# RWKV-7 key norms as a two-part float32r product, with the norm's scale put into B

## The chip, the cores and the metric

The kernel runs on one core of a Trainium2 chip. The metric is the device time of one execution in microseconds. The kernel before took 2318.72 us, the median of 3 runs (2318.38 to 2319.49). PE is the matrix engine, DVE the vector engine, ACT the scalar engine, POOL and SP the other two; PEld stands for PE's weight loads. Products that the code makes in float32r carry the label f32 in the profile; the kernel splits such an operand into two float32r parts, "hi" (a cast) and "lo" (what the cast left over).

## The reference, cut to what matters

A layer of 1024 tokens by 2048 features: an RMS norm, one input projection, two groups of heads (RWKV-7 and HGRN2), one output projection, a residual and a last RMS norm. The change lies in the RWKV-7 group, 16 heads of 64 channels:

```python
kk = (k * k_k).reshape(B, T, H, N)
kk = kk / jnp.maximum(jnp.linalg.norm(kk, axis=-1, keepdims=True), 1e-12)
k = k * (1.0 + (a - 1.0) * k_a)
...
avec = -kk
bvec = kk * a4

def step(S, inp):
    rt, wt, kt, vt, at, bt = inp
    Sa = jnp.einsum('bhvk,bhk->bhv', S, at)
    S = S * wt[:, :, None, :] + Sa[..., None] * bt[:, :, None, :] + vt[..., None] * kt[:, :, None, :]
    y = jnp.einsum('bhvk,bhk->bhv', S, rt)
    return S, y
```

In the product of avec and bvec the norm of kk appears squared: 1/max(|kk|², 1e-24) per token and head, times -1. The kernel keeps kk without its norm and applies that one factor somewhere, with another factor 0.5 because sigmoid is made from tanh: a = (1 + tanh)/2.

## The kernel before, in words

**Tiling.** Activations lie with features on the 128 partitions and tokens along the free dimension, 512 tokens ("half" 0 and 1) at a time. A tile of 128 partitions holds two RWKV heads, so the 16 heads are 8 pairs `i`, and each part below runs 16 times (8 pairs, 2 halves). 512 tokens are 8 chunks of 64.

**The product that everything else rides on.** `gemm` makes one block of 128 output columns of the input projection: 16 slices of the contraction, three matmuls each (lines 780, 781, 782: hi by hi, hi by lo, lo by hi). Weights come by DMA (`raw`), ACT casts them (`whi`, line 743) and DVE subtracts (`wlo`, line 753), three parts of four slices ahead of use. After each slice, that is after every three matmuls, `gemm` calls `step()`, which lets every waiting lane run up to its next `yield`. So the order of the instructions on each engine is written out by the counts of yields (the constants F00 to F06 and R00 to R20): a "step" is three matmuls of the projection plus what the lanes put behind them. Each pair takes 8 blocks, K, R, V, four for HGRN2 and the RWKV gate, which is 128 steps. Pair 0 of each half has two blocks more, for the low-rank inputs.

**The lane `front`** (`rwkv_front`) is queued when block K is taken out of PSUM, and starts three steps later (six steps after the second low-rank block for pair 0). I count its steps as f0, f1 and so on:

- f0: ACT makes `kk` (line 427) and its square `ksq` (429).
- f1: PE makes the decay product `pz` with `product` (line 188, three matmuls), ACT its tanh (435); then PE makes the squared norms `pn` with four plain float32 matmuls (439) in which the weights are slices of `ksq` and the moving operand is two columns of the block matrix, so that the tokens come out on partitions.
- f2: DVE adds 1 (444) and makes the cumulative sum `G` over each chunk (449).
- f4: PE makes the rate product (188, three matmuls), ACT its tanh `tha` (454); DVE makes `D2`, -2/max(norm², 1e-24), 128 partitions by 8 columns (458 four times, 459).
- f5: ACT makes `Em` (462) and `km` (464). f7: DVE line 466. f9: DVE makes `ab` (469). f11 to f17: DVE makes `BK` in four pieces (474).

**The lane `rwkv`** (`rwkv_scan`) is queued when block V is taken out, 32 steps after K, takes what the front left, and needs 116 steps. It makes products of `BK` with `LH` (line 515), scales one part by `D2` into `PA` (522), inverts a triangular matrix, and from its step 83 on goes through the 8 chunks, four steps each. I write c0 to c3 for the steps of one chunk:

- c0: PE 650 and 651 (which need the state `X`), ACT copies `R` (653), POOL makes `SW` (656).
- c1: PE 659, then DVE 660 and ACT 661 scale by `D2` into `X`.
- c3: PE 665 (which needs 660 and 661), DVE 667 twice (the next chunk's state), PE 670, ACT 672.
- The next chunk's c0 follows one step after c3; its line 650 needs line 667.

The front of pair i starts 96 + 3 = 99 steps after block V of the pair before was taken out, that is at step 99 of the pair before's scan, which is c0 of its fifth chunk (99 - 83 = 16). So f0, f4 and f8 are steps c0, f1, f5 and f9 are c1, f3, f7 and f11 are c3. This holds for 14 of the 16 fronts; the front of pair 0 has no chunk loop beside it in either half. A lane queued earlier comes first within a step: the chunk loop's instructions stand before the front's.

The helpers that the change calls, and the line in the class that sets the weights it uses:

```python
def halves(self, name, src, tags=(None, None)):
    shape = list(src.shape)
    return tuple(self.sp.tile(shape, F32R, name=name + n, tag=t or name + n) for n, t in zip("hl", tags))

def product(self, ps, w, x):
    pairs = [(a, b) for a, b in ((0, 0), (0, 1), (1, 0)) if a < len(w)]
    for n, (a, b) in enumerate(pairs):
        self.nc.tensor.matmul(ps, lhsT=w[a], rhs=x[b], start=n == 0, stop=n == len(pairs) - 1)

def halving(self, hi, lo, src):
    self.nc.scalar.copy(hi, src)
    yield
    self.nc.vector.tensor_tensor(lo, src, hi.bitcast(F32), op=ALU.subtract)
```

`self.ones` is the 128x128 block matrix in float32r: ones where row and column belong to the same head.

Of the kernel before, what the change touches and what calls it, by code (L numbers as in the profile page):

```python
# [13 lines left out]
AF = mybir.ActivationFunctionType  # L14
ALU = mybir.AluOpType
AX = mybir.AxisListType

P = 128
# [7 lines left out]
C0 = math.exp(-0.5)  # L26
# [13 lines left out]
CID, CPK, CBO, CRS, CIQ, NCST = 0, 128, 256, 384, 896, 1152  # L40
# [38 lines left out]
class Layer:  # L79
# [340 lines left out]
    def rwkv_front(self, i, k, thwd, adm, wh, got):  # L420

        nc, sp, cst = self.nc, self.sp, self.cst
        one = lambda tile_, off=0: tile_[:, off + i : off + i + 1]
        ch = lambda x: x.rearrange("p (c t) -> p c t", t=64)
        hp = (slice(0, 64), slice(64, P))
        kk = self.tmp("kk", tag="kk")
        nc.scalar.activation(kk, k, AF.Copy, scale=one(self.vec, VKK))
        ksq = self.tmp("ksq")
        nc.scalar.activation(ksq, kk, AF.Square)
        yield from range(F00)  # L430

        pz = self.pm()
        self.product(pz, [w[:, 0, :] for w in wh], thwd)
        thw = self.tmp("th", 2)
        nc.scalar.activation(thw, pz, AF.Tanh, scale=0.5, bias=one(self.hw0))

        pn = self.pm()
        for j in range(4):
            nc.tensor.matmul(
                pn[:, 2 * j : 2 * j + 2], lhsT=ksq[:, P * j : P * j + P], rhs=cst[:, CBO : CBO + P : 64],  # L440
                start=True, stop=True,
            )
        yield from range(F01)
        nc.vector.tensor_scalar_add(thw, thw, 1.0)

        if self.YG is None:
            self.YG = sp.tile([P, 2, HT], F32, name="Y", tag="L")
        G = self.YG[:, 1, :]
        nc.vector.tensor_tensor_scan(G, cst[:, CRS : CRS + HT], thw, initial=0.0, op0=ALU.mult, op1=ALU.add)
        yield from range(F02)  # L450
        pz = self.pm()
        self.product(pz, [w[:, 1, :] for w in wh], adm)
        tha = self.tmp("tha", tag="ksq")
        nc.scalar.activation(tha, pz, AF.Tanh, scale=0.5, bias=one(self.ha0))
        D2 = self.tmp("D2", 2, 8)
        for h in (0, 1):
            for e in (0, 1):
                nc.vector.tensor_scalar(D2[hp[h], e:8:2], pn[hp[e], h:8:2], 1e-24, -2.0, op0=ALU.max, op1=ALU.mult)
        nc.vector.reciprocal(D2, D2)
        yield from range(F03)  # L460
        Em = self.tmp("Em")
        nc.scalar.activation(Em, G, AF.Exp, scale=0.5 * C0)
        km = self.tmp("km")
        nc.scalar.activation(km, tha, AF.Identity, scale=one(self.hka), bias=one(self.oka))
        yield from range(F04)
        nc.vector.tensor_tensor(km, km, k, op=ALU.mult)
        yield from range(F05)
        ab = k
        nc.vector.scalar_tensor_tensor(ab, tha, 1.0, kk, op0=ALU.add, op1=ALU.mult)
        yield from range(F05)  # L470
        BK = sp.tile([P, 8, P], F32, name="BK")
        for x, flip in ((ab, 0), (km, 1)):
            for h in (0, 1):
                nc.vector.tensor_tensor(BK[hp[h], :, hp[h ^ flip]], ch(x)[hp[h]], ch(Em)[hp[h]], op=ALU.mult)
                yield from range(F06)
        got["front"] = kk, km, G, D2, BK

    def rwkv_scan(self, i, half, r, v, got, lsc, xsc, y):
        nc, sp, ident, cst = self.nc, self.sp, self.ident, self.cst
# [3 lines left out]
        hp = (slice(0, 64), slice(64, P))  # L483
# [7 lines left out]
        X = sp.tile([P, 9, P], F32, name="Xs")  # L491
# [6 lines left out]
            nc.gpsimd.memset(LH[hp[1 - h], :, 0, hp[h]], 0.0)  # L498
        while "front" not in got:
            yield  # L500
        kk, km, G, D2, BK = got.pop("front")
        nc.scalar.activation(Ep[:, :, 1:65], ch(G), AF.Exp, scale=-0.5 * C0)
        yield from range(R00)
        for e, z in enumerate((kk, r)):
# [5 lines left out]
        PA = sp.tile([P, 8, 64], F32, name="PA", tag="PA")  # L510
        PR = sp.tile([P, 8, P], F32, name="PR", tag="PR")
        for q in range(4):
            pp = self.pm()
            for c in (2 * q, 2 * q + 1):
                nc.tensor.matmul(  # L515
                    pp[:, (c % 2) * 256 : (c % 2 + 1) * 256], lhsT=BK[:, c, :], rhs=LH[:, c].rearrange("p x n -> p (x n)"),
                    start=True, stop=True,
                )
            cs = slice(2 * q, 2 * q + 2)
            pv = pp.rearrange("p (c x h t) -> p c x h t", c=2, x=2, h=2)  # L520
            for h in (0, 1):
                nc.vector.tensor_tensor(
                    PA[hp[h], cs, :], pv[hp[h], :, 0, h, :], D2[hp[h], cs].unsqueeze(2).broadcast_to([64, 2, 64]), op=ALU.mult
                )
                nc.vector.tensor_tensor(
                    LH[hp[1 - h], cs, 0, hp[h]], pv[hp[1 - h], :, 0, h, :],
                    cst[hp[1 - h], CPK + 64 : CPK + P].unsqueeze(1).broadcast_to([64, 2, 64]), op=ALU.mult,
                )
            nc.vector.tensor_tensor(
                PR[:, cs, :].rearrange("p c (h t) -> p (c h) t", h=2), pp.rearrange("p (c x h t) -> p c x h t", c=2, x=2, h=2)[:, :, 1],  # L530
                cst[:, CPK : CPK + 64].unsqueeze(1).broadcast_to([P, 4, 64]), op=ALU.mult,
            )
            yield from range(R09)
# [112 lines left out]
        for c in range(8):  # L646
            j, e = c // 2, c % 2
            wc = Ep[:, c, 64:65]
            ps, py = self.pc(), self.pc()[:, 0:P]
            nc.tensor.matmul(ps[:, 0:P], lhsT=LH[:, c, 0, :], rhs=X[:, c, :], start=True, stop=True)  # L650
            nc.tensor.matmul(py, lhsT=LH[:, c, 1, :], rhs=X[:, c, :], start=True, stop=False)
            R = sp.tile([P, P], F32, name="R")
            nc.scalar.copy(R, ps[:, 0:P])  # L653
            SW = sp.tile([P, 64], F32, name="SW")
            for h in (0, 1):
                nc.gpsimd.tensor_scalar_mul(SW[hp[h], :], X[hp[h], c, hp[h]], wc[hp[h]])  # L656
            yield from range(R18)
            pu = ps[:, P : 2 * P]
            nc.tensor.matmul(pu, lhsT=TT[:, c, :], rhs=R, start=True, stop=True)  # L659
            nc.vector.tensor_scalar_mul(X[hp[0], c, hp[0]], pu[hp[0], hp[0]], D2[hp[0], c : c + 1])  # L660
            nc.scalar.activation(X[hp[1], c, hp[1]], pu[hp[1], hp[1]], AF.Copy, scale=D2[hp[1], c : c + 1])  # L661
            yield from range(R19)
            if c < 7 or half == 0:
                pq = ps[:, 2 * P : 3 * P]
                nc.tensor.matmul(pq, lhsT=BKt[:, c, :], rhs=X[:, c, :], start=True, stop=True)  # L665
                for h in (0, 1):
                    nc.vector.scalar_tensor_tensor(  # L667
                        X[hp[h], c + 1, hp[h]], pq[hp[h], hp[h]], wc[hp[h]], SW[hp[h], :], op0=ALU.mult, op1=ALU.add
                    )
            nc.tensor.matmul(py, lhsT=PR[:, c, :], rhs=X[:, c, :], start=False, stop=True)  # L670
            for h in (0, 1):
                nc.scalar.copy(Y[hp[e], j, hp[h]], py[hp[h], hp[h]])  # L672
            yield from range(R20)
# [646 lines left out]
```

## Time and profile before

| | |
|---|---|
| time, median of 3 runs | 2318.72 us (2318.38 to 2319.49) |
| the profiled execution: its time | 2318.71 us |
| the profiled execution: its span | 2316.9 us |
| PE busy | 2289.8 us |
| PE weight loads busy | 1893.5 us |
| DVE busy | 1449.2 us |
| ACT busy | 982.6 us |
| POOL busy | 428.9 us |
| mean granted clock of PE | 0.997 |

The span is counted from the first to the last instruction; 1.8 us of the execution lie around it. "Busy" adds up overlapping records, and the ends of matmuls are modelled, so PE's rate is better read from the starts of its matmuls or from the chain of waits, which gives each instruction only the time by which it moved the end. A group's line gives code line, engine, operation, the tiles (out<-in), their shapes and counts, then busy time, mean ns of one and the idle time before it.

### The profile page before, as it was taken

What the parts mean: (1) busy time and instruction counts of PE and PEld (TensorE: products, weight loads), DVE (VectorE), ACT (ScalarE), POOL (GpSimd) and SP (SyncE); (2) the same over time, 40 slices, a digit from 0 to 9 for tenths busy, and PEclk for the clock granted to TensorE, in tenths of its full rate; (3) what the DMA queues carried; (4) which work ended last, traced back from release to release, by engine and by line L of the source; (5) the groups of instructions that cost most, each with busy time, mean ns of one, the idle gap of its engine ahead of it and who ended that gap; (6) DMA issues with size and microseconds to landing.
All of it is one profiled execution on the core that took longest, in us unless ns stands there. A gap on an engine that the chain in (4) does not pass through costs nothing.

```text
span 2316.9 us, 34790 instructions
## 1 busy us (share of the span) xinstructions
PE 2289.8 (99%) x12555; PEld 1893.5 (82%) x12555; DVE 1449.2 (63%) x3136; ACT 982.6 (42%) x2284; POOL 428.9 (19%) x826
## 2 busy tenths in 40 slices
PE   8999999999999999999999999999999999999998
PEld 6888888888888888778888888888888887888888
DVE  5566666667676766757575757576757677436333
ACT  5344444444343434553434343434344445324323
POOL 3021212122121212230202020202121214001000
PEclk9999999999999999999999999999999999999999
DMA  6333434343435262624242424242424244434722
GB/s 180 75 111 86 114 84 117 85 119 83 113 99 133 78 144 64 178 71 96 70 107 70 107 70 108 70 107 70 107 70 107 71 106 142 182 118 137 260 95 100
DMA packets 379660, 249.37 MB, mean 108 GB/s; under 512 B 54368, under 2 KB 346464, under 8 KB 378336
## 3 DMA queue, kind: packets, MB, share of 16 engines
q1 hardware_dynamic: 372000, 230.37, 37.8%
q10 hardware_dynamic: 6912, 12.59, 1.7%
q0 software_dynamic: 576, 4.19, 0.4%
q8 instruction: 99, 1.62, 0.3%
q14 instruction: 73, 0.60, 0.1%
HBM read 221.15 MB, written 25.95 MB: 107 GB/s over the span
## 4 chain that ended last, share of the span: by engine, by line
PE 92%; DVE 3%; issue 2%; ACT 1%; POOL 1%; DMA 1%; SPq 0%; POOLq 0%; ACTq 0%; DVEq 0%
PE g L780 20%; PE g L782 20%; PE g L781 20%; PE m L515 2%; PE m L284 2%; PE c L795 2%; PE c L793 2%; PE c L794 2%; PE m L795 1%; PE m L794 1%; PE m L793 1%; PE c L659 1%; PE m L188 1%; PE c L650 1%; PE g L793 1%
## 5 line engine op out<-in xcount | busy, mean ns | idle before, releaser
L780 PE MATMUL g<-xs,whi 128*128 128x512 f32 (+1 forms) x2160 | 903.3, 418 | 0.0
L782 PE MATMUL g<-xs,wlo 128*128 128x512 f32 (+1 forms) x2160 | 846.9, 392 | 0.5 <-DVE wlo L753 0.5
L781 PE MATMUL g<-xs,whi 128*128 128x512 f32 (+1 forms) x2160 | 843.9, 391 | 0.0
L753 DVE TENSOR_TENSOR wlo<-raw,whi 128x512 fp32r<-128x512 f32 (+1 forms) x646 | 449.1, 699 | 294.8 <-ACT whi L743 293.9
L743 ACT CAST whi<-raw 128x512 fp32r<-128x512 f32 (+1 forms) x648 | 395.2, 618 | 395.5 <-PE g L781 230.1
L782 PEld LDWEIGHTS g<-xs,wlo 128*128 128x128 f32 (+1 forms) x2160 | 403.7, 187 | 92.1 <-DVE wlo L753 1.4
L780 PEld LDWEIGHTS g<-xs,whi 128*128 128x128 f32 (+1 forms) x2160 | 405.4, 188 | 75.1
L781 PEld LDWEIGHTS g<-xs,whi 128*128 128x128 f32 (+1 forms) x2160 | 405.9, 188 | 66.8
L656 POOL TENSOR_SCALAR SW<-Xs,Ep 64x64 f32<-64x64 f32 x256 | 137.2, 536 | 262.6 <-DVE Xs L667 251.0
L597 DVE TENSOR_TENSOR Xw<-L,X 128x32 f32<-128x32 f32 (+15 forms) x256 | 114.6, 448 | 9.9 <-POOL L L592 5.0
L601 DVE TENSOR_REDUCE X<-Xw 128x16 f32<-128x32 f32 (+15 forms) x256 | 111.7, 436 | 8.8
L672 ACT COPY Y<-c 64x64 f32<-64x64 f32 x256 | 53.0, 207 | 137.1 <-PE c L670 133.7
L660 DVE TENSOR_SCALAR Xs<-c,D 64x64 f32<-64x64 f32 x128 | 35.2, 275 | 121.2 <-PE c L659 105.9
L667 DVE SCALAR_TENSOR_TENSOR Xs<-c,Ep,SW 64x64 f32<-64x64 f32 x240 | 67.3, 281 | 56.8 <-PE c L665 51.4
L311 POOL TENSOR_TENSOR hqp<-hqp,tot 128x256 f32<-128x256 f32 x96 | 67.8, 706 | 174.2 <-ACT hq L335 85.4
L585 POOL MEMSET L<- 128x16 f32 x32 | 3.0, 137 | 484.9 <-DMA L<-lsc 375.1
L554 ACT COPY Xs<-m 64x256 f32<-64x256 f32 x64 | 23.5, 368 | 145.1 <-PE m L551 117.2
L615 POOL COPY PX<-Xr 32x256 f32<-32x256 f32 x32 | 12.7, 396 | 340.1 <-DVE Xr L613 339.4
L661 ACT ACTIVATE Xs<-c,D 64x64 f32<-64x64 f32 x128 | 39.6, 310 | 68.1 <-DVE Xs L660 67.3
L753 POOL TENSOR_TENSOR xs<-xn,xs 128x512 fp32r<-128x512 f32 x24 | 35.1, 1467 | 179.0 <-DMA xn<-y 106.1
L653 ACT COPY R<-c 128x128 f32<-128x128 f32 x128 | 33.9, 265 | 78.1 <-PE c L650 78.1
L659 PEld LDWEIGHTS c<-R,TT 128*128 128x128 f32 x256 | 46.6, 188 | 24.0 <-POOL SW L656 12.2
(511 smaller groups left out, 3475.0 us busy)
## 6 DMA issues: line engine op xcount, KB each, us to landing
raw<-in_w_in SPq DMA_DIRECT2D x256, 512.0 KB
raw<-in_w_out SPq DMA_DIRECT2D x64, 512.0 KB
L<-lsc SPq DMA_DIRECT2D x16, 512.0 KB
xr<-in_x SPq DMA_DIRECT2D x32, 256.0 KB
xn<-y ACTq DMA_DIRECT2D x32, 256.0 KB
out<-h SPq DMA_DIRECT2D x16, 512.0 KB
xr<-in_x SPq DMA_DIRECT2D x8, 512.0 KB
y<-yt SPq DMA_DIRECT2D x16, 256.0 KB
```

Of the source, the lines that this page charges most:

```text
L597: nc.vector.tensor_tensor(w[:, :, :, 0:n], Lp[:, k, :, 2 * k :].unsqueeze(1).broadcast_to([P, 8, 2, n]), Xi[:, :, 2 * k :].unsqueeze(2).br ...
L601: nc.vector.tensor_reduce(Xi[:, :, 2 * k : 2 * k + 2].unsqueeze(3), w[:, :, :, 0:n], axis=AX.X, op=ALU.add)
L656: nc.gpsimd.tensor_scalar_mul(SW[hp[h], :], X[hp[h], c, hp[h]], wc[hp[h]])
L659: nc.tensor.matmul(pu, lhsT=TT[:, c, :], rhs=R, start=True, stop=True)
L743: nc.scalar.copy(hi[:, :, 0:n], raw)
L753: low()
L780: nc.tensor.matmul(ps[e], lhsT=hi[:, k, 0:n], rhs=x[:, 0, :], start=kk == 0, stop=False)
L781: nc.tensor.matmul(ps[e], lhsT=hi[:, k, 0:n], rhs=x[:, 1, :], start=False, stop=False)
L782: nc.tensor.matmul(ps[e], lhsT=lo[:, k, 0:n], rhs=x[:, 0, :], start=False, stop=kk == NK - 1)
L793: mm(ps, lhsT=x[:, 0, ts], rhs=hi, start=first, stop=False)
L794: mm(ps, lhsT=x[:, 0, ts], rhs=lo, start=False, stop=False)
L795: mm(ps, lhsT=x[:, 1, ts], rhs=hi, start=False, stop=last)
```

## The change

It makes the squared norms another way and applies their reciprocal in another place.

- The square `ksq` is split into two float32r parts (`kh`, in the buffers of `km` and `Em`), and the norms come from `product` with the block matrix as weights: two matmuls of 512 columns. The norms now lie like the keys, channels on partitions and one column per token, each repeated over the 64 partitions of its head. The split takes two steps; what followed f0 comes two steps later.
- Instead of the 128x8 `D2`, a 128x512 tile `kr` (in the buffer of `Em`) holds the reciprocal of the norms: a maximum out of PSUM and a reciprocal, both on DVE.
- `ab` is multiplied by -0.5 and `kr` in a second DVE instruction; `Em` is made after that, one step later, because `kr` has its buffer.
- `PA` and the two updates of `X` become plain copies.

```diff
+        kh = self.halves("kn", ksq, ("km", "Em"))
+        yield from self.halving(*kh, ksq)
+        yield
 
         pz = self.pm()
         self.product(pz, [w[:, 0, :] for w in wh], thwd)
...
         pn = self.pm()
-        for j in range(4):
-            nc.tensor.matmul(
-                pn[:, 2 * j : 2 * j + 2], lhsT=ksq[:, P * j : P * j + P], rhs=cst[:, CBO : CBO + P : 64],
-                start=True, stop=True,
-            )
+        self.product(pn, [self.ones], kh)
         yield from range(F01)
...
-        D2 = self.tmp("D2", 2, 8)
-        for h in (0, 1):
-            for e in (0, 1):
-                nc.vector.tensor_scalar(D2[hp[h], e:8:2], pn[hp[e], h:8:2], 1e-24, -2.0, op0=ALU.max, op1=ALU.mult)
-        nc.vector.reciprocal(D2, D2)
+
+        kr = self.tmp("kr", tag="Em")
+        nc.vector.tensor_scalar_max(kr, pn, 1e-24)
+        nc.vector.reciprocal(kr, kr)
         yield from range(F03)
-        Em = self.tmp("Em")
-        nc.scalar.activation(Em, G, AF.Exp, scale=0.5 * C0)
         km = self.tmp("km")
...
         nc.vector.scalar_tensor_tensor(ab, tha, 1.0, kk, op0=ALU.add, op1=ALU.mult)
+        nc.vector.scalar_tensor_tensor(ab, ab, -0.5, kr, op0=ALU.mult, op1=ALU.mult)
+        yield
+        Em = self.tmp("Em")
+        nc.scalar.activation(Em, G, AF.Exp, scale=0.5 * C0)
         yield from range(F05)
...
-                nc.vector.tensor_tensor(
-                    PA[hp[h], cs, :], pv[hp[h], :, 0, h, :], D2[hp[h], cs].unsqueeze(2).broadcast_to([64, 2, 64]), op=ALU.mult
-                )
+                nc.vector.tensor_copy(PA[hp[h], cs, :], pv[hp[h], :, 0, h, :])
...
-            nc.vector.tensor_scalar_mul(X[hp[0], c, hp[0]], pu[hp[0], hp[0]], D2[hp[0], c : c + 1])
-            nc.scalar.activation(X[hp[1], c, hp[1]], pu[hp[1], hp[1]], AF.Copy, scale=D2[hp[1], c : c + 1])
+            nc.vector.tensor_copy(X[hp[0], c, hp[0]], pu[hp[0], hp[0]])
+            nc.scalar.copy(X[hp[1], c, hp[1]], pu[hp[1], hp[1]])
```

So in the new front the steps are: f0 `kk` and `ksq`; f1 the cast; f2 the subtraction; f3 the decay product, its tanh and the norms; f4 the addition and the cumulative sum; f6 the rate product, its tanh, the maximum and the reciprocal; f7 `km`; f9 line 466's product; f11 the two instructions on `ab`; f12 `Em`; f14 to f20 `BK`. The front ends three steps later than before.

More of the change, by code (lines that the diff above doesn't have):

```diff
@@ L475, in rwkv_front @@
                 yield from range(F06)
-        got["front"] = kk, km, G, D2, BK
+        got["front"] = kk, km, G, BK
     def rwkv_scan(self, i, half, r, v, got, lsc, xsc, y):
@@ L500, in rwkv_scan @@
             yield
-        kk, km, G, D2, BK = got.pop("front")
+        kk, km, G, BK = got.pop("front")
         nc.scalar.activation(Ep[:, :, 1:65], ch(G), AF.Exp, scale=-0.5 * C0)
```

## The prediction

> **What bounds the kernel now.** I read the page's head first, then the chain of work that ended last, then who waited for whom, then the timeline of one front.
>
> ```profile
> span 2316.9 us, 34790 instructions
> ...
> PE 2289.8 (99%) x12555; PEld 1893.5 (82%) x12555; DVE 1449.2 (63%) x3136; ACT 982.6 (42%) x2284; POOL 428.9 (19%) x826
> ...
> PEclk9999999999999999999999999999999999999999
> ...
> PE 92%; DVE 3%; issue 2%; ACT 1%; POOL 1%; DMA 1%; SPq 0%; POOLq 0%; ACTq 0%; DVEq 0%
> ...
> L782 PE MATMUL g<-xs,wlo 128*128 128x512 f32 (+1 forms) x2160 | 846.9, 392 | 0.5 <-DVE wlo L753 0.5
> ...
> PEld c L650 <- DVE Xs L667: 19.7, 78, 1.0
> ...
> PEld c L665 <- ACT Xs L661: 6.9, 18, 0.4
> ```
>
> PE is busy in 99% of the span at full clock and carries 92% of the chain, so time put on PE's queue counts in full, and time on DVE counts only where PE then waits. The big supply from DVE, `wlo`, is hardly ever waited for (0.5 us in all): it runs three parts ahead, and a part is twelve matmuls. The tight place is the chunk loop: PE's line 650 waited 78 times for DVE's line 667, one step before it. A DVE instruction that stands in front of 667 has almost no cover.
>
> **PE's side of the change.** The chain of waits over one front (pair 4, half 0; start, time in the chain, what):
>
> ```profile
> 642.14 0.71 PE m L188 x3
> 642.85 0.90 PE m L439 x8
> 643.75 0.34 PE g L780
> 644.09 0.23 PE g L781
> ```
>
> The four float32 matmuls of the norms are eight records and take 0.90 us, and the matmul behind them 0.34 instead of 0.23. Three float32r matmuls of 512 columns take 0.71, so two take 0.47. Net: 0.90 + 0.11 - 0.47 = **0.54 us less per front**. The wait for the square is inside these figures:
>
> ```profile
>   ACT ksq L429: 4.0, 14
> ...
> 1033.81 0.95 PE L439 MATMUL m<-cst,ksq 128*128 128x2 f32 x8
> 1034.62 0.49 PE L780 MATMUL g<-xs,whi 128*128 128x512 f32 x1
> 1034.95 0.40 PE L781 MATMUL g<-xs,whi 128*128 128x512 f32 x1
> ```
>
> The first row is the wait of line 439 (4.0 us in 14 fronts). In a front of pair 0, without the chunk loop, nothing is waited for: 0.81 us from 439 to 780, and 0.33 to the next instead of 0.23, so 0.81 + 0.10 - 0.47 = 0.44 us less. On PE alone the change is worth 14 x 0.54 + 2 x 0.44 = **8.4 us**. The new norms wait for the split: cast at f1, subtraction at f2, used at f3 behind the decay product's 0.71 us. I cost that at nothing; the cover is one step (three matmuls, 0.7 us) and that product against 0.69 us of DVE.
>
> **DVE's side.** Rows of the groups, and below them two of the start of the kernel:
>
> ```profile
> L459 DVE RECIPROCAL D<-D 128x8 f32<-128x8 f32 x16 | 3.2, 203 | 0.5
> ...
> L458 DVE TENSOR_SCALAR D<-m 64x4 f32<-64x4 f32 x64 | 10.2, 160 | 0.8
> ...
> L315 DVE TENSOR_TENSOR tot<-tot 128x8 f32<-128x8 f32 x16 | 2.5, 158 | 0.0
> ...
> L444 DVE TENSOR_SCALAR th<-th 128x512 f32<-128x512 f32 x16 | 6.8, 427 | 9.5 <-ACT th L435 9.5
> ...
> L449 DVE TENSOR_TENSOR_SCAN Y<-cst,th 128x512 f32<-128x512 f32 x16 | 19.6, 1225 | 0.6
> ...
> L254 DVE SCALAR_TENSOR_TENSOR hg<-th,g 128x512 f32<-128x512 f32 x16 | 10.9, 679 | 0.0
> ...
> L702 DVE SCALAR_TENSOR_TENSOR yr<-m,vec,bv 128x512 f32<-128x512 f32 x16 | 12.0, 750 | 1.0 <-PE m L700 0.5
> ...
> L229 DVE TENSOR_TENSOR rkl<-ksq,rkh 128x512 fp32r<-128x512 f32 x16 | 11.0, 685 | 0.0
> ...
> L107 DVE TENSOR_SCALAR omu<-vec 128x2 f32<-128x2 f32 x1 | 0.2, 163 | 0.0
> ```
>
> Added per front: a subtraction (0.69, line 229), a maximum out of PSUM (0.70, estimated between 679 ns from SBUF and 750 from PSUM), a reciprocal of 512 columns, and a second product on `ab` (0.68). Removed: 4 x 0.16 + 0.20 = 0.84.
>
> The reciprocal of 512 columns, R, is the number that decides, and the trace has it only at 8 columns. It took 203 ns, where the other instructions of its size take about 160. If the 45 ns are a fixed extra, R is between 0.43 (line 444's rate) and 0.73 (0.68 and 45 ns). If they are paid per column, it is long: over the 163 ns of two columns they are 5.0 ns a column and R = 0.16 + 2.56 = 2.7 us; over a fixed part of 150 (line 315's 158 less 8 columns at 1.0 ns, which is (679 - 158)/504) they are 6.6 ns and R = 0.15 + 3.39 = 3.5. With nothing fixed it would be 203/8 x 512 = 13 us, which the two-column row speaks against. Line 449 shows that DVE has operations above 1 ns a column (1225 ns, over 2 ns a column). I take the middle of the two fits, **R = 3.1 us**, because equal small operations differ by some 10 ns only, and let the range go to 4.5, where the fixed part would be some 135 ns.
>
> [...]
>
> **Where the reciprocal stands.** It is issued at f6, which is chunk step c2: behind 660 (f5) and the `wlo` of that place, ahead of 667 (f7); PE's 650 of the next chunk is at f8. The timeline of that stretch (start, time, engine, line):
>
> ```profile
> 647.86 0.82 ACT L370 COPY AT<-AD 64x256 f32<-64x256 f32 x2
> ...
> 648.71 0.69 ACT L454 ACTIVATE tha<-m,ha 128x512 f32<-128x512 f32 x1
> ...
> 648.87 0.38 PE L659 MATMUL c<-R,TT 128*128 128x128 f32 x2
> ...
> 649.30 0.61 ACT L743 CAST whi<-raw 128x512 fp32r<-128x512 f32 x1
> 649.36 0.28 DVE L660 TENSOR_SCALAR Xs<-c,D 64x64 f32<-64x64 f32 x1 [1.49 <-PE c L659]
> ...
> 649.94 0.69 DVE L753 TENSOR_TENSOR wlo<-raw,whi 128x512 fp32r<-128x512 f32 x1 [0.31 <-ACT whi L743]
> ...
> 650.90 0.60 DVE L667 SCALAR_TENSOR_TENSOR Xs<-c,Ep,SW 64x64 f32<-64x64 f32 x2 [0.26 <-PE c L665]
> ...
> 652.06 0.38 PE L650 MATMUL c<-Xs,LH 128*128 128x128 f32 x2
> ...
> 656.11 0.58 DVE L667 SCALAR_TENSOR_TENSOR Xs<-c,Ep,SW 64x64 f32<-64x64 f32 x2 [0.48 <-PE c L665]
> ...
> 656.83 0.41 PE L650 MATMUL c<-Xs,LH 128*128 128x128 f32 x2
> ```
>
> I replay it with the new order. PE is 0.54 us earlier. ACT's cast 743 no longer stands behind `tha` (moved from f4 to f6), so it follows line 370: 647.86 + 0.82 - 0.54 = 648.14. The `wlo` subtraction starts 0.64 after it, as here: 648.78. (660 is no later: 659 loses 0.54 and the moved rate product's 0.71 in front of it, and the addition and cumulative sum of f4 end by about 648.3.) `wlo` 0.67, maximum 0.70: the reciprocal starts at 650.15 and ends at 650.15 + R. Then 667, and 650 starts 0.72 behind 667's start, as in the last two rows, where it also waited for 667: 650.87 + R. Before it started at 652.06. So a front costs **R - 1.2 us**; PE stalls from R = 0.65 on, and the gain is used up at R = 1.2. The same working gives R - 1.2 in pair 2 of half 0 and in pair 3 of half 1, and R - 1.7 in pair 5 of half 0, where four transposes of another lane lie in between.
>
> What waits behind the reciprocal: 667, then `wlo` with its parts in hand, then the front's own 466 three steps on. ACT's share (one cast of 0.6 us more, `Em` later) lies beside PE.
>
> **The other edits.** The pair on `ab` stands behind 667 at f11 and ahead of 660 at f13; two steps are 1.4 us of matmuls and the pair 1.36, so up to 0.4 us a front may stick out: nothing in the sum, 5 us in the range. The front ends 22 steps after its start instead of 19, and starts 3 steps (pair 0: 6) after block K (the second low-rank block); 25 or 28 is still below the 32 at which the scan asks for it, so nothing is late; without that cover a step costs 0.7. The scalings that become copies:
>
> ```profile
> L661 ACT ACTIVATE Xs<-c,D 64x64 f32<-64x64 f32 x128 | 39.6, 310 | 68.1 <-DVE Xs L660 67.3
> ...
> L672 ACT COPY Y<-c 64x64 f32<-64x64 f32 x256 | 53.0, 207 | 137.1 <-PE c L670 133.7
> ```
>
> 661 gets 0.1 us shorter; PE waited for it 18 times, so at most 1.8 us, of which I count 1. Copies 660 and 522 lie between a gain of 0.1 and nothing; counted as nothing.
>
> **Sum.** Fronts beside a chunk loop: 14 x (3.1 - 1.2) = +26.6. Pair 0, twice, where no 667 stands behind the reciprocal: -0.9. Line 661: -1. Together +24.7 us on the profiled 2318.71 us (span 2316.9 and 1.8 around it), which is the median too: **2343 us**.
>
> **Rivals.** (a) *The reciprocal streams* like DVE's other operations, 0.43 to 0.73 us, its 45 ns being fixed. For it: one size cannot tell fixed from per column. Against it: other small operations of quite different kinds stand within 10 ns of each other. Then 650 waits for nothing that counts, and the change keeps PE's 8.4 and 661's 1 us: 2309 us, faster. It decides below R = 1.2. (b) *The reciprocal goes at the cumulative sum's rate*, 1.2 us: the stall eats the gain, 14 x 0, and the 2 us of the rest leave 2317 us, within what can be told from no change. [...]
>
> **Chances.** A measurement of this kernel tells about 0.2%, 4.6 us, from no change, that is R within some 0.3 us of 1.3. The forecast 0.52 and (c) 0.20, together a cost per column, with an own range of 2333 (14 x 1.3 - 2 with a little below the fit of 2.7) to 2364 (R = 4.5); (b) with its surroundings 0.06; (a) 0.22. To leave out no more than 2 in 10 the range has to take in (a), which alone holds more: 2307 to 2364. Slower 0.72, the same 0.06, faster 0.22.
>
> **What would show it.** The reciprocal's row: 2.5 to 4.5 us, 16 times. PE's wait of 650 for DVE's 667: from 20 us to some 50. Line 439's eight records gone, two of 512 columns in their place, 0.23 apart; DVE busy up by 16 x (2.07 + R - 0.84), some 69 us, to 1518. The forecast is wrong if the reciprocal's row is below 1.5 us, or if it is long and 650 does not wait behind it.

## The result, and the profile after

The changed kernel takes 2361.06 us (median of 5 runs, 2355.51 to 2363.86), the one before 2319.49 (5 runs, 2318.38 to 2320.73): a ratio of 1.0171, 95% interval 1.0159 to 1.0182. It is 41.6 us slower. The forecast was 2343, with a range of 2307 to 2364. The profiled execution took 2363.86 us, 45 more than the profiled one before. The head of its page:

```profile
span 2362.1 us, 34625 instructions
## 1 busy us (share of the span) xinstructions
PE 2297.4 (97%) x12459; PEld 1891.3 (80%) x12459; DVE 1515.9 (64%) x3120; ACT 976.9 (41%) x2300; POOL 424.3 (18%) x826
...
PE 83%; DVE 7%; ACT 3%; issue 2%; DMA 2%; POOL 1%; SPq 0%; POOLq 0%; ACTq 0%; DVEq 0%
```

PE has 96 instructions less and its share of the chain falls from 92% to 83%; DVE's rises from 3 to 7, ACT's from 1 to 3. The lines behind the norm code move: 648, 663 and 665 are the 650, 665 and 667 of before, 658 and 659 the 660 and 661, and 751 and 778 to 780 the 753 and 780 to 782. The groups that answer to the ones of before (busy us, mean ns):

```profile
L457 DVE RECIPROCAL kr<-kr 128x512 f32<-128x512 f32 x16 | 53.6, 3353 | 0.6
...
L456 DVE TENSOR_SCALAR kr<-m 128x512 f32<-128x512 f32 x16 | 10.9, 680 | 0.0
...
L522 DVE COPY PA<-m 64x128 f32<-64x128 f32 x128 | 36.3, 284 | 12.1 <-PE m L515 11.5
...
L658 DVE COPY Xs<-c 64x64 f32<-64x64 f32 x128 | 27.4, 214 | 104.2 <-PE c L657 79.1 <-POOL hq L340 21.9 <-POOL hqp L311 1.0
...
L659 ACT COPY Xs<-c 64x64 f32<-64x64 f32 x128 | 26.5, 207 | 64.3 <-DVE Xs L658 63.1
```

The reciprocal of 512 columns takes 3.35 us. And who waited for whom:

```profile
PE c L648 <- DVE Xs L665: 33.8, 17, 2.9
...
PEld c L648 <- DVE Xs L665: 57.8, 92, 3.3
PEld c L663 <- ACT Xs L659: 11.0, 35, 0.5
```

PE and its weight loads now wait 33.8 and 57.8 us for line 665 (1.5 and 19.7 before; the two overlap and are not to be added). The 78 waits that the prediction gives to line 650 are those of its weight loads. The chain of waits in the front that the prediction replayed shows the path (half 0; the prediction calls it pair 4, but counted from 0 it is the front of pair 5, beside the chunk loop of pair 4):

```profile
660.09 0.63 ACT whi L741
660.72 0.03 issue
660.74 0.69 DVE wlo L751
661.43 0.61 DVE kr L456
662.05 0.02 issue
662.07 3.35 DVE kr L457
665.42 0.10 DVE Xs L665
665.52 0.03 issue
665.55 0.30 DVE Xs L665
665.85 0.04 issue
665.89 0.49 PE c L648 x2
```

For seven microseconds (from 658.79 to 665.89) nothing of PE is on the chain: four short ACT instructions that are left out here, ACT's cast, four DVE instructions and the moments between them, and then line 648.

The distance from one front's first instruction (line 427) to the next front's tells what a front costs. Against the kernel before, seven of these distances are longer by 2.2 to 2.4 us, and six by 3.5 to 5.3. The two that hold a front of pair 0 changed by +0.2 and -0.7. The six longer ones are those in which the granted clock falls to half. Two fronts beside each other, first the timeline (one row of each), then windows of the first (length, busy of PE, PEld, DVE, ACT, POOL, then the granted clock, DMA, GB/s):

```profile
665.89 0.49 PE L648 MATMUL c<-Xs,LH 128*128 128x128 f32 x2 [2.29 <-DVE Xs L665]
...
1415.22 0.49 PE L648 MATMUL c<-Xs,LH 128*128 128x128 f32 x2 [2.29 <-DVE Xs L665]
```

```profile
664.00:666.00 2.00, 0.11 (x1) 0.11 (x1) 1.81 (x3) 0.25 (x1) 0.06 (x1) 1.00 0.00 0
666.00:668.00 2.00, 2.00 (x10) 1.81 (x11) 0.00 (x0) 0.78 (x2) 1.03 (x3) 0.73 0.00 0
668.00:670.00 2.00, 2.00 (x8) 1.71 (x8) 1.51 (x3) 0.21 (x1) 0.00 (x0) 0.50 0.00 0
670.00:672.00 2.00, 2.00 (x14) 1.83 (x14) 0.67 (x3) 0.12 (x1) 0.00 (x0) 0.92 0.00 0
1415.00:1419.00 4.00, 3.78 (x24) 3.37 (x25) 2.01 (x5) 0.99 (x3) 0.88 (x2) 1.00 0.02 4
```

Both fronts have the same gap, 2.29 us. Behind the first the clock is at half for 3.4 us (2 x 0.27 + 2 x 0.50 + 2 x 0.08 = 1.7 us lost, which at half speed is 3.4 us), behind the second it stays full. Cut into windows of 1 us, the six spells lie at 544, 666, 789, 912, 1175 and 1772 us; the profile before is at half clock only from 13.2 to 20.0 us and in its last 6.5 us, which hold no front (the profile here likewise from 11.5 to 18.4 us and in its last 5.6).

### The profile page after: what moved, and what is told of

It is laid out like the page before. It is cut to its first block, busy times and chain, and to the rows that moved or that the text cites. A ratio compares the mean times of both kernels' runs of the same rounds, so it can differ in the third digit from the quotient of the medians.

```text
span 2362.1 us, 34625 instructions
## 1 busy us (share of the span) xinstructions
PE 2297.4 (97%) x12459; PEld 1891.3 (80%) x12459; DVE 1515.9 (64%) x3120; ACT 976.9 (41%) x2300; POOL 424.3 (18%) x826
## 4 chain that ended last, share of the span: by engine, by line
PE 83%; DVE 7%; ACT 3%; issue 2%; DMA 2%; POOL 1%; SPq 0%; POOLq 0%; ACTq 0%; DVEq 0%
PE g L778 18%; PE g L780 18%; PE g L779 18%; PE m L515 2%; PE m L284 2%; DVE kr L457 2%; PE c L791 2%; PE c L793 2%; PE c L792 2%; PE m L792 1%; PE m L791 1%; PE m L793 1%; PE c L648 1%; PE g L791 1%; PE g L792 1%
## 5 line engine op out<-in xcount | busy, mean ns | idle before, releaser
L654 POOL TENSOR_SCALAR SW<-Xs,Ep 64x64 f32<-64x64 f32 x256 | 129.4, 506 | 311.2 <-DVE Xs L665 299.3
L658 DVE COPY Xs<-c 64x64 f32<-64x64 f32 x128 | 27.4, 214 | 104.2 <-PE c L657 79.1
L648 PEld LDWEIGHTS c<-Xs,LH 128*128 128x128 f32 x256 | 41.0, 189 | 61.1 <-DVE Xs L665 57.8
L648 PE MATMUL c<-Xs,LH 128*128 128x128 f32 x256 | 54.8, 296 | 33.8 <-DVE Xs L665 33.8
```

## The experiments

The theories before the first runs. **A**: the reciprocal ahead of line 665 costs everything, through PE's wait and through the half-clock spells that follow the wait. **B**: a good part comes from the change's other work on DVE and from the later end of the front. All edits are to the changed kernel unless said otherwise; ratios are to the kernel before on the same chip.

**No reciprocal.**

```diff
-        nc.vector.reciprocal(kr, kr)
+        nc.vector.tensor_scalar(kr, kr, 0.0, 3e-4, op0=ALU.mult, op1=ALU.add)
```

> The changed kernel with the reciprocal left out: in its place DVE writes a constant over the same 128x512 tile (some 0.43 us instead of 3.35), so the keys are not normalised. Theory A (the reciprocal in front of line 665 costs everything, through PE's wait and through the half-clock spells that follow it): no wait of PE's line 648 beyond that of before, no half-clock spell within the fronts, and PE's gain is left: 2309 us (2306 to 2313). Theory B (a good part of the loss comes from the other DVE work, the second product on ab and the subtraction, or from the later end of the front): above 2320 us.

Measured: 2316.47 us, ratio 0.9987 (0.9978 to 0.9997). Between the two: the loss is gone and no front has a half-clock spell, but most fronts gain only 0.1 to 0.3 us where PE's work became 0.54 us shorter (pair 0, without a chunk loop: 0.5). The chain of the front at 1370 us shows one place where the rest stays:

```profile
1385.53 0.61 DVE k__13450 L465
1386.14 0.02 issue
1386.16 0.71 DVE k__13450 L466
1386.87 0.02 issue
1386.89 0.40 ACT Em L469
1387.29 0.14 issue
1387.43 0.60 ACT whi L741
1388.03 0.02 issue
1388.06 0.22 ACT Xs L659
1388.27 0.04 issue
1388.32 0.49 PE c L668 x2
```

The new second product on `ab` (466) holds up `Em`, which had to move behind it for the sake of the buffer; `Em` stands on ACT ahead of the cast 741 and of the chunk loop's 659, and PE's 668 needs 659. That is theory C, tested below.

**More work for PE in the gap.**

```diff
         yield from range(F03)
+        pd = self.pm()
+        for _ in range(8):
+            nc.tensor.matmul(pd, lhsT=self.ones, rhs=kh[0], start=True, stop=True)
         km = self.tmp("km")
```

> The changed kernel with eight matmuls of 512 columns more in each front, at f7, results unused: 1.9 us of work for PE in the stretch in which it waits for the reciprocal. Theory A (after a gap of some 2.3 us the clock falls to half for 3.4 us in some fronts, 1.7 us each): the gap shrinks to 0.5 us, the six spells inside the fronts are gone, and the kernel gets faster by having more work: 2351 us (2347 to 2354). Theory B (the excess over the wait comes from elsewhere): 2361 us or, with 14 x 1.9 us that do not fit the gap, up to 2388.

Measured: 2356.03 us, ratio 1.0159 (1.0143 to 1.0174), about 5 us below the changed kernel's 2361.06 although PE has 128 matmuls more. The intervals of the two ratios overlap, so the times alone do not show that it is faster, and 2356 lies outside theory A's range; the profile shows more. Every distance between fronts with a chunk loop is now longer by 1.8 to 2.9 us, most by 2.4; none by 4. The same place of the same front:

```profile
665.07 0.49 PE L651 MATMUL c<-Xs,LH 128*128 128x128 f32 x2 [0.42 <-DVE Xs L668]
```

Here 651 is the 648 of the changed kernel. The wait is 0.42 us instead of 2.29, the end of the reciprocal still sets the time, and no spell lies within the fronts. So the spells are a cost of their own: six of them with gaps of 1.85 to 2.89 us in the fronts, none with the gap filled. The saving of 5 us lies below the 10 of the profile with six spells, for two reasons: the two distances that hold a front of pair 0, where there is no such gap to fill, grew by 1.1 and 1.9 us, and by their mean clocks (0.993 to 0.996) the changed kernel's runs do not all have six.

**The reciprocal one step later, behind line 665.**

```diff
         nc.vector.tensor_scalar_max(kr, pn, 1e-24)
-        nc.vector.reciprocal(kr, kr)
         yield from range(F03)
+        nc.vector.reciprocal(kr, kr)
         km = self.tmp("km")
```

> The changed kernel with the same reciprocal issued one step later, at f7, so that it stands behind DVE's line 665 and not ahead of it. Theory A (its place ahead of 665 decides): the next deadline is line 658, two steps on, which has some 1.2 us to spare at 663; reciprocal 3.35 us from 665's end, so 658 about 1.2 us late and 665 of the next chunk 0.7 late: 2318 us (2311 to 2326), no half-clock spell in the fronts. Theory B (DVE has no room for 3.4 us in a chunk, wherever it stands): 2340 us or more.

Measured: 2322.45 us, ratio 1.0014 (1.0004 to 1.0023); 0.1 to 0.4 us a front, no spell in the fronts. The same instructions on the same engine, one place later in the queue, and 39 of the 42 us are gone. Theory A holds in kind; it was 4 us too hopeful.

**The reciprocal in pieces behind the chunk loop's instructions.** 256 columns at f7, 128 ahead of the `km` product at f9, 128 ahead of `ab` at f11:

```diff
-        nc.vector.reciprocal(kr, kr)
...
+        nc.vector.reciprocal(kr[:, 0:256], kr[:, 0:256])
         km = self.tmp("km")
...
+        nc.vector.reciprocal(kr[:, 256:384], kr[:, 256:384])
         nc.vector.tensor_tensor(km, km, k, op=ALU.mult)
         yield from range(F05)
+        nc.vector.reciprocal(kr[:, 384:512], kr[:, 384:512])
         ab = k
```

> The changed kernel with the reciprocal in three pieces behind the chunk loop's DVE instructions: 256 columns at f7, 128 at f9, 128 at f11 (1.75, 0.95 and 0.95 us at 6.25 ns a column and 0.15 fixed). Theory A: each fits between two deadlines of the chunk loop, PE keeps its gain: 2311 us (2307 to 2317), faster than before. Theory B (the 70 us that DVE does more are paid wherever they stand): 2330 us or more.

Measured: 2327.13 us, ratio 1.0034 (1.0022 to 1.0045): a miss, worse than the whole reciprocal at f7, 0.3 to 0.8 us a front. The chain of the front at 1374 us runs through DVE without a break from f9 on:

```profile
1389.46 0.91 DVE kr L462
1390.37 0.55 DVE km L463
1390.92 0.60 DVE wlo L753
1391.51 0.26 DVE hst L389
1391.77 0.24 DVE Xs L667
```

From f9 to f12 DVE is full (660, the `km` product, a `wlo`, another lane's `hst`, 667), so a piece put there pushes back what follows: the chain runs on through the third piece, the pair on `ab`, `Em` and ACT's cast to PE's line 670 at 1396.30. The two pieces, 0.91 and 0.86 us, cost some 0.75 us a front against the kernel without the reciprocal. In this kernel PE waited 6.4 and 5.7 us in all for ACT's 661 (659 in the changed kernel).

**`Em` behind line 659,** on the kernel without the reciprocal:

```diff
-        yield
+        yield from range(2)
         Em = self.tmp("Em")
```

> The changed kernel with the reciprocal left out (a constant is written in its place, so the keys are not normalised) and Em made one step later, at f13, behind ACT's line 659 and not ahead of it. The kernel without the reciprocal alone gave 2316.5 us, 0.4 us a front short of PE's gain. Theory C: 0.26 us of that is PE's wait at f15 for 659, which stands on ACT behind Em, which waits for DVE's second product on ab; it goes, so 2313 us (2311 to 2315). Theory D: the second product itself, or the earlier waits at f3, hold PE: 2316 us as without the move.

Measured: 2312.83 us, ratio 0.9968 (0.9956 to 0.9981). Theory C: most fronts now gain 0.4 to 0.6 us, what the prediction worked out for PE alone (0.54). One yield was worth about 0.35 us a front.

**Both moves together:** the whole reciprocal at f7 and `Em` at f13.

> The changed kernel with the whole reciprocal one step later (f7, behind line 665) and Em one step later (f13, behind ACT's 659). The first alone gave 2322.5 us. Theory C: the wait at f15 goes here too, 0.3 to 0.4 us a front: 2317.5 us (2315 to 2320). Theory D: as the first alone, 2322.

Measured: 2316.68 us, ratio 0.9985 (0.9976 to 0.9994); -0.3 to +0.3 us a front. As theory C had it.

**Nothing long from f9 to f12:** 384 columns at f7, 128 with the products on `ab` at f13, `Em` at f15.

```diff
-        nc.vector.reciprocal(kr, kr)
...
+        nc.vector.reciprocal(kr[:, 0:384], kr[:, 0:384])
         km = self.tmp("km")
...
-        yield from range(F05)
+        yield from range(2 * F05)
+        nc.vector.reciprocal(kr[:, 384:512], kr[:, 384:512])
         ab = k
...
-        yield
+        yield from range(2)
         Em = self.tmp("Em")
```

> The changed kernel with 384 columns of the reciprocal at f7, 128 at f13 behind line 658 together with both products on ab, and Em at f15, so that no long DVE work stands in the full stretch from f9 to f12. Theory A and C together: PE waits no more than in the kernel before and keeps 0.4 us a front: 2313 us (2310 to 2316), faster than before. Rival: DVE is full between the chunk loop's instructions, and what is taken from f9 to f12 comes out late after f13: 2318 us or more.

Measured: 2319.21 us, ratio 1.0000 (0.9991 to 1.0008). The rival holds: the chunk loop is free of it, but what was moved lies later among DVE's work, and the next scan's first products now wait for DVE, 0.43 us each time on average.

```profile
PE m L516 <- DVE LH L507: 5.6, 13, 0.6
```

(516 is the product 515 of `BK` with `LH`; in the kernel before, PE does not wait for `LH` there.)

**Only the reciprocal, in the kernel before.**

```diff
-        yield from range(F04)
+        yield
+        nc.vector.reciprocal(thw, thw)
+        yield
```

> The kernel before, unchanged but for one 128x512 reciprocal of a tile that is no longer used, issued at the step of chunk place c2 in which the change has its own (behind line 660 and the wlo of that place, ahead of 667). Nothing else of the change is in it. Theory A: by the replay 650 starts 650.61 + 3.35 + 0.72 = 654.68 instead of 652.06, 2.6 us a front, 14 times 36.7, and half-clock spells of 1.7 us in some six fronts: 2366 us (2358 to 2372). Theory B (the change's other edits are needed for the loss): below 2345 us.

Measured: 2359.49 us, ratio 1.0167 (1.0153 to 1.0181). One instruction per front, with nothing else of the change, loses as much as the whole change: most fronts 2.3 to 2.5 us, four with a half-clock spell 4.0 to 4.3.

```profile
PE c L652 <- DVE Xs L669: 31.8, 17, 2.8
```

(652 and 669 are the 650 and 667 of the kernel before.) Theory B falls.

**Two more places.** 384 columns at f7 and 128 at f11, `Em` at f13; and 64 at f6, 384 at f7, 64 at f11, `Em` at f13. The second:

```diff
         nc.vector.tensor_scalar_max(kr, pn, 1e-24)
-        nc.vector.reciprocal(kr, kr)
+        nc.vector.reciprocal(kr[:, 0:64], kr[:, 0:64])
         yield from range(F03)
+        nc.vector.reciprocal(kr[:, 64:448], kr[:, 64:448])
         km = self.tmp("km")
...
         yield from range(F05)
+        nc.vector.reciprocal(kr[:, 448:512], kr[:, 448:512])
         ab = k
...
-        yield
+        yield from range(2)
         Em = self.tmp("Em")
```

> The changed kernel with 384 columns of the reciprocal at f7, 128 at f11 ahead of the products on ab, Em at f13. At 6.25 ns a column the 384 take 2.55 us and end before line 658 is due; the 128 (0.95 us) and the pair stand in front of 658 of the last chunk, which has 1.2 us to spare. Theory: 0.1 to 0.3 us a front better than with the whole reciprocal at f7: 2314.5 us (2312 to 2317). Rival: the stretch f11 to f13 is as full as f9 to f11, no gain over 2316.7.

> As the one before, but 64 columns at f6 ahead of line 665 (0.55 us, below the 0.65 us by which the replay lets the reciprocal hold 665 up without PE waiting), 384 at f7, 64 at f11. Theory: 2313.5 us (2311 to 2317). Rival: 665 is what PE waits for most often, so even 0.55 us in front of it costs: 2318 us or more.

Measured: 2318.25 us, ratio 0.9995 (0.9986 to 1.0004), a miss; and **2314.62 us, ratio 0.9977 (0.9967 to 0.9987)**, 0.2% faster than the kernel before. In the second most fronts gain 0.3 to 0.6 us, so most of PE's gain is kept. In the first twice as many columns, 128, stand ahead of the pair on `ab`: its chain runs through them and the pair to 658 and 659 of the last chunk.

## Why the prediction was right, and where it was not

**The deciding step held.** The prediction said that the reciprocal would be paid per column, stand ahead of line 667 (665 after) and make PE's 650 (648) wait. It did, in the 14 fronts beside a chunk loop and in neither of pair 0.

**R was 3.35 us, not 3.1:** between the two fits, 2.7 and 3.5. That is 0.25 x 14 = 3.5 us of the error.

**The replay held.** It put the reciprocal's start 8.90 us after the front's first instruction (650.15 - 641.25) and line 648, with R = 3.35, 12.97 after it. The chain above has 9.1 and 12.9 (662.07 and 665.89, the front starting at 653.0). So line 648 comes 2.09 us later than 650 did before, where R - 1.2 is 2.15; beside the four transposes (the front at 776 us) it is 1.56, where R - 1.7 is 1.65.

**What failed is the sum, in two terms.** The first is "14 x (3.1 - 1.2) = +26.6": it counted the wait and took PE to run at full speed behind it. In six of the 14 fronts it ran at half clock for 3.4 us, 1.7 us each, about 10 us of the profiled 45. The kernel before shows no such spell in a front, and there line 650 waited at most 0.6 us for 667 (its weight load at most 1.0).

The second is "ACT's share (one cast of 0.6 us more, `Em` later) lies beside PE". `Em` lay in front of 659 on ACT's queue and waited for the new product: about 0.35 us a front, some 5 us, by the two pairs of kernels with `Em` at f12 and at f13. The changed kernel has this wait too: in its front at 291 us, line 663 at f15 falls back by another 0.25 us. The prediction had kept up to 0.4 us a front for that product in its range, but looked for it at DVE's 660, not at ACT.

**The tally of the profiled 45.2 us of span:** 14 fronts at 2.35, +32.9; six spells at 1.7, +10.2; pair 0, about -0.5 by the two distances. That is 42.6. Of the 2.6 that are left 1.9 come behind the last front; their cause is not shown. Against the forecast of 24.7: R adds 3.5, the spells 10.2, pair 0 0.4 and what is left 2.6. The other 3.8 lie in the fronts, where `Em` is the one cause shown. All the errors go the same way, so none hid another.

**The rivals.** (a), the streaming reciprocal, and (b) fell with its row. The chance of 0.20 for (c) stood for a column dearer than both fits. No run shows such a price: 6.25 ns were measured, between the fits' 5.0 and 6.6. The range held the time, near its upper end; but that end stood for an R of 4.5 us, not for a slowed clock or a wait for ACT, so this was in part luck.

**PE's side** was right: 0.54 us less a front, 0.4 to 0.6 measured in most fronts once both waits were out of the way, with the shorter 661 in it. In the changed kernel's time nothing of it is left.

**Copies.** 658 went from 275 to 214 ns and 659 from 310 to 207, 522 stayed at 284, all within the bounds given.

## What to carry to other kernels

DVE ran 665 here only when the reciprocal in front of it had ended (662.07 + 3.35 = 665.42 us). In such a queue, price a new long instruction by the first deadline that stands behind it, not by the engine's free share: DVE was busy 63% before and 64% after, and one place in its queue decided about 39 us (2361.06 against 2322.45). Ask the same of what is moved for the sake of a buffer, on every engine it passes. Before turning a value from 8 columns into 512, look for operations whose cost per column is high (the reciprocal's 6.25 ns here), and where PE sets the time, count what a gap costs afterwards as well as the gap (1.7 us more in six of 14 fronts here).

## What the hardware showed that was not expected

**DVE's reciprocal took 6.25 ns a column and 0.15 us.** The pieces of the kernels above give the line; of 128x384, 128x256 and 128x64 (the first and last from the kernel with 64, 384 and 64):

```profile
L459 DVE RECIPROCAL kr<-kr 128x384 f32<-128x384 f32 x16 | 40.8, 2551 | 0.4
...
L457 DVE RECIPROCAL kr<-kr 128x64 f32<-128x64 f32 x16 | 8.8, 553 | 0.6
```

```profile
L458 DVE RECIPROCAL kr<-kr 128x256 f32<-128x256 f32 x16 | 28.0, 1752 | 0.4
```

From 256 to 512 columns it is (3353 - 1752)/256 = 6.25 ns, and 0.15 + 8 x 6.25 ns is the 203 ns of the 8 columns before. The maximum of 512 columns out of PSUM took 680 ns.

**In six of the 14 fronts PE's clock was at half for 3.41 us behind the gap, and the gap's length did not tell which.** Twelve of the fronts have a gap of 2.29 us, and four of these were hit; the other two that were hit have 1.85 and 2.89. The clock's record in the trace tells more. In the profiled execution all its changes lie whole multiples of 3.413 us apart: the six spells begin at 544.02, 666.90, 789.78, 912.66, 1175.49 and 1772.82 us, that is 36, 36, 36, 77 and 175 times 3.413 us from one to the next. The trace can be cut into cells on this grid. The first two cells below are those of the front at 653 us: its gap lies in one cell, and the next cell runs at half clock. The gap at 1413 us is divided between the other two, and the clock stays (columns as in the windows above):

```profile
663.49:666.90 3.41, 1.12 (x7) 0.93 (x7) 2.32 (x3) 1.24 (x4) 0.87 (x2) 1.00 0.00 0
666.90:670.32 3.42, 3.42 (x14) 3.02 (x13) 1.51 (x3) 0.51 (x2) 0.22 (x2) 0.50 0.00 0
1411.00:1414.42 3.42, 1.93 (x13) 1.41 (x11) 3.38 (x2) 2.14 (x5) 0.00 (x0) 1.00 0.00 0
1414.42:1417.83 3.41, 2.61 (x16) 2.33 (x17) 1.55 (x6) 0.99 (x3) 0.88 (x2) 1.00 0.02 5
```

Five of the six fronts that were hit had more than 2.1 us of their gap in one cell, the sixth 1.85; the eight others had at most 1.95. In the kernel before with nothing but the reciprocal added it is 1.96 to 2.15 for the four that were hit and at most 1.68 for the others. With the gap filled down to 0.42 us (1.02 at most) no front was hit. The idle time is not the only measure: in the kernel without the reciprocal a gap of 1.31 us behind the last front, next to sixteen matmuls of 64 columns, was followed by a spell too. The grid falls differently from one profile to the next: the clock first falls to half at 11.54 us in the changed kernel and at 13.19 in the kernel before, 1.64 us or about half a cell apart. From this I estimate that the number of fronts that are hit differs from run to run. The run times fit that: the changed kernel's five runs lie 8.4 us apart, with a mean clock of 0.993 in the slowest and of 0.995 and 0.996 in the two fastest.
